# Reordering the first loads and splits, the last tile's gate, and the loads of stored activations and gate chunks in a PEER decoder layer

## Chip, cores and metric

One NeuronCore of a Trainium2 chip runs the kernel; the metric is the device time of one execution in microseconds (us), as the median of several runs. The profile is one further execution, taken by the hardware profiler.

## What is computed

One layer of a decoder for 512 prompt rows and 64 sample rows of width 1024, in float32. The layer is a combined input projection, attention and a spatial gating unit, an expert layer (PEER), and a last gate. Cut to what the change touches:

```python
xn = rmsnorm(x);  z = xn @ w_in                 # q, k, v, su, sv, two gates
...                                              # attention, gating unit, merge -> x1
q = rmsnorm(x1) @ w_q                            # 8 heads, scores against 2 x 128 sub keys
idx, gate = top16 of the 128 x 128 experts       # per row and head
w = gate * gelu(sum(u[idx] * rmsnorm(x1)))
x2 = x1 + sum(w * v[idx])                        # u, v: 16384 experts x 1024
gate2 = sigmoid(rmsnorm(x2) @ w_ple_gate)
x3 = x2 + gate2 * (p @ w_ple)
```

## The kernel before

**Precision.** Every float32 product is made of three fp32r matmuls. `split` (line 65) writes the high half of an operand with an activation copy on ACT and the rest with a subtraction on DVE. `load_block` (line 69) loads a weight block of 512 KB into `w_raw` (4 buffers), and splits it into `w_hi` and `w_lo` (3 buffers each). `tform` (line 78) runs high x high, high x low, low x high for each of eight blocks of 128 input rows, accumulating in a PSUM bank.

**Order.** The program text is not the order in which the engines run. A planner puts the instructions of each engine's queue in order while it works through a model of the run. Of those whose inputs and buffers are free it takes the one that stands first in the text; `tc.high_priority(offset=n)` moves an instruction n places ahead in that ranking. A load whose buffer is free can thus be issued long before its place in the text. Each queue then runs strictly in the order it was given. All plain loads and stores are issued by SP.

**Head** (lines 169 to 197). SP loads a small vector tile, then x transposed in eight blocks `xT` of 128 x 576, with the first block of `w_in` after the second of them, then `ident`. For each block ACT squares it and DVE adds the square into `tot` (`add`, ranked 500 ahead). ACT makes `xn[0]` (the high half of x times the norm's gain) and DVE `xn[1]` (the rest). `rstd_rows` turns `tot` into `rn`, the reciprocal norm of each column. `w_chunk` c multiplies `w_in` block c with all of x in two column halves (`HALVES`, 256 and 320 columns), one after the other, each in one of the two `mm` banks of PSUM, and DVE multiplies the result by `rn` on its way out. Nine small constants are loaded between chunk 0 and chunk 1. There are 30 chunks.

**Middle.** After the merge, the top-16 search runs mainly on DVE while TensorE does stage 1: for each expert block j of 128 (`stage1`, line 762) the activations of all 128 experts of that block for 384 prompt rows. The activations of j = 2, 4, ..., 38 (`SPILL`) are written to DRAM (`ad`), those of 43 others stay on chip. `build_g` (line 799) builds the dense gate of every expert and row and stores it in DRAM (`gd`). The other 192 rows get their experts by row gathers on GpSimd.

**Stage 2** (lines 943 to 985). For j = 0 to 127: load the block of `peer_v`, multiply the activations of block j by the gate (line 974, on DVE), split them into `wh` and `wl` (2 buffers each), and run 18 matmuls into six `oacc` banks (`stage2`, line 935). While stage 1 blocks are left, one is run beside; for j below 40 beside every second block. At block j the spilled activations of block j + 2 are loaded from `ad` into one of three `x1c` buffers (line 946). Every eighth block the gate of eight blocks (1.5 MB) is loaded as one chunk `gsl` (line 966); two chunks have a buffer.

**Tail** (lines 986 to 1027). Five row tiles are normalized, turned by TensorE (`tail_turn`, through `mm` banks) and multiplied by `w_ple_gate`. In `tail_gate` (line 898) the two column halves of 512 take turns, 48 matmuls in all. `tail_out` (line 905) then loads the tile's `pl`, and for each half takes the sigmoid on ACT, two DVE operations, and stores.

Of the kernel before, what the change touches and what calls it, by code (L numbers as in the profile page):

```python
# [7 lines left out]
F32 = mybir.dt.float32  # L8
# [3 lines left out]
AF = mybir.ActivationFunctionType  # L12
ALU = mybir.AluOpType
# [4 lines left out]
P = 128  # L18
D = 1024
NT = 576  # L20
NB = 384
KC = 8
NS = 64
NJ = 128
TB = 16
JB = 8
GP = [0.5, 0.0, 1.65]
G2 = (1.6, 2.0)
SPILL = set(range(2, 40, 2))
# [12 lines left out]
HALVES = (slice(0, 256), slice(256, 576))  # L42
# [5 lines left out]
def tile_decoder_step(ctx: ExitStack, tc: tile.TileContext, a, o):  # L48
    nc = tc.nc
    V, A, T, G, S = nc.vector, nc.scalar, nc.tensor, nc.gpsimd, nc.sync  # L50
# [9 lines left out]
    def cload(name, shape, pl=None):  # L60
        t = (pl or const).tile(shape, F32, name="c_" + name, bufs=1)
        S.dma_start(t, a[name])
        return t

    def split(src, hi, lo):
        A.activation(hi, src, AF.Copy)  # L66
        V.tensor_sub(lo, src, hi.bitcast(F32))  # L67

    def load_block(src, shape=(P, KC, P)):
        raw = wp.tile(list(shape), F32, name="w_raw", bufs=4)  # L70
        S.dma_start(raw, src)
        hi = wp.tile(list(shape), F32R, name="w_hi", bufs=3)
        lo = wp.tile(list(shape), F32R, name="w_lo", bufs=3)
        with tc.high_priority(offset=1000):
            split(raw, hi, lo)
        return hi, lo

    def tform(ps, w, x, wk=0, nk=KC):
        n, i = 3 * nk, 0
        for k in range(nk):  # L80
            for wi, xi in ((0, 0), (0, 1), (1, 0)):
                mark_pe[0] = T.matmul(ps, lhsT=w[wi][:, wk + k, :], rhs=x[xi][k], start=i == 0,  # L82
                                   stop=i == n - 1)
                i += 1
# [7 lines left out]
    def mm():  # L92
        return psM.tile([P, 512], F32, name="mm")
# [7 lines left out]
    pld = dr.tile([NT, D], F32, name="pld")  # L101
    ad = dr.tile([NSP, P, NB], F32, name="ad")
    gd = dr.tile([NJ // JB, P, NB // TB, JB, TB], F32, name="gd")
# [15 lines left out]
    def f8(mk, *args):  # L119
        t = [mk(*args), mk(*args)]  # L120
        return [t[k // 4][:, k % 4, :] for k in range(KC)]
# [4 lines left out]
    def bank(tag):  # L126
        return psB.tile([P, 512], F32, name=tag)

    def joint(w, x, out, wk=0, nk=KC, bk=mm):
        for cols in HALVES:  # L130
            ps = bk()[:, :cols.stop - cols.start]
            tform(ps, w, [[xi[k][:, cols] for k in range(nk)] for xi in x], wk, nk)
            out(ps, cols)

    def sumsq():
        tot = e1.tile([P, NT], F32, name="rstd", bufs=1)

        def add(k, x):
            sq = tt() if k else tot
            A.activation(sq, x, AF.Square)  # L140
            if k:
                V.tensor_tensor(tot, tot, sq, op=ALU.add)
            if k == KC - 1:
                A.activation(eps[:, 2:3], sq[:, 0:1], AF.Sqrt)
        return tot, add
# [22 lines left out]

    vecs = cload("vecs", [P, 18])
    xT = f8(f4)  # L170
    for k in range(KC):
        S.dma_start(xT[k], a["xT"][k])
        if k == 1:
            first = load_block(a["w_in"][0])
    ident = cload("ident", [P, P])
    xn = (f8(x4), f8(x4))
    tot, add = sumsq()
    for k in range(KC):
        with tc.high_priority(offset=500):
            add(k, xT[k])  # L180
        A.activation(xn[0][k], xT[k], AF.Copy, scale=vecs[:, k:k + 1])  # L181
        V.scalar_tensor_tensor(xn[1][k], xT[k], vecs[:, k:k + 1], xn[0][k].bitcast(F32),
                               op0=ALU.mult, op1=ALU.subtract)
    rn = e1.tile([P, NT], F32, name="rn", bufs=1)
    with tc.high_priority(offset=500):
        for cols, ps in rstd_rows(tot, lambda: bank("sc")):
# [2 lines left out]
    def w_chunk(c, dst, out):  # L189
        def scaled(ps, cols):  # L190
            with tc.high_priority(offset=1000):
                V.tensor_tensor(dst[:, cols], ps, rn[:, cols], op=ALU.mult)
            out(cols)
        joint(load_block(a["w_in"][c]) if c else first, xn, scaled)

    kraw, vTr = tt(), tt()
    w_chunk(0, kraw, lambda cols: None)
# [40 lines left out]
    for g in range(4):  # L238
# [7 lines left out]
        if g == 0:  # L246
            pv = bank("pt")
# [3 lines left out]
            pv = bank("pt")  # L251
# [206 lines left out]
    for i in range(24):  # L458
        if i < 8:
            t, g = (svT, suT)[i // 4], i % 4  # L460
            z = t[:, g, :]
            w_chunk(6 + i, z, lambda cols: A.activation(z[:, cols], z[:, cols], AF.Gelu_apprx_tanh))
        else:
            c, br = divmod(i - 8, 2)
            if (i - 8) % 4 == 0:
                sg4.append(f4())
            sg = sg4[-1][:, (i - 8) % 4, :]
# [15 lines left out]
    hs = ([], [])  # L483
    for c in range(KC):
        w = load_block(a["w_br"][c])
        for i, (x, k0_) in enumerate(((ahl, 0), (mhl, 4))):
            sg = sgs[2 * c + i]
# [20 lines left out]
    for c in range(KC):  # L508
        w = load_block(a["w_out"][c])
# [18 lines left out]
    for c0, r in tilesA:  # L528
# [4 lines left out]
        for hh in range(2):  # L533
            hs = slice(hh * 512, (hh + 1) * 512)
            pt = bank("pt")
            for k in range(4):
                x1k = x1[hh * 4 + k][:, c0:c0 + r]
                T.transpose(out=pt[:r, k * P:(k + 1) * P], in_=x1k, identity=ident)
                if r == NS:
# [3 lines left out]
                                   op0=ALU.mult, op1=ALU.mult)  # L543
# [186 lines left out]
    for i in range(16):  # L730
        h, c = i // 4 + i % 2 * 4, i // 2 % 2
        w = load_block(a["peer_wq"][2 * h + c])
# [17 lines left out]
    def pay(x):  # L750
        credit[0] += x
        n = int(credit[0])
        credit[0] -= n
        gather(n, mark_pe[0])
# [42 lines left out]
    gsp = [pool(gs_s, "gsp%d" % i, 1) for i in range(2)]  # L797
# [40 lines left out]
    for tb in range(NB // TB):  # L838
        if tb == TBK:
# [7 lines left out]
            g0 = late.tile([P, JB, TB], F32, name="g0")  # L847
# [19 lines left out]
    d3 = pool(ds, "d3", 3)  # L867
    gsp = [pool(ds, "gsl%d" % i, 1) for i in range(2)]
# [26 lines left out]
    def tail_scale(x2, ss, r, xn3):  # L895
        V.scalar_tensor_tensor(xn3[:r], x2[:r], ss[:r], pg[:r], op0=ALU.mult, op1=ALU.mult)

    def tail_gate(w, xh, xl, r, ps):
        for k in range(KC):
            for xi, wi in ((xh, 0), (xh, 1), (xl, 0)):  # L900
                for hh in range(2):
                    T.matmul(ps[hh][:r], lhsT=xi[:, k, :r], rhs=w[k][wi][:, hh * 512:(hh + 1) * 512],  # L902
                             start=k == 0 and xi is xh and wi == 0, stop=k == KC - 1 and xi is xl)

    def tail_out(x2, r, c0, ps, sg, pl):
        S.dma_start(pl[:r], pld[c0:c0 + r])
        for hh in range(2):
            hs = slice(hh * 512, (hh + 1) * 512)
            A.activation(sg[:r, hs], ps[hh][:r], AF.Sigmoid)
            V.tensor_tensor(sg[:r, hs], sg[:r, hs], pl[:r, hs], op=ALU.mult)  # L910
            V.tensor_tensor(sg[:r, hs], sg[:r, hs], x2[:r, hs], op=ALU.add)
            S.dma_start(o["y"][c0:c0 + r, hs], sg[:r, hs])
# [27 lines left out]
                                      start=j == 0 and last == 0 and vi is vh, stop=j == NJ - 1 and last == 1)  # L940

    tails, spp, back = [], [], {}
    for j in range(NJ):
        if j + 2 in SPILL:
            back[j + 2] = d3.tile([P, NB], F32, name="x1c")
            S.dma_start(back[j + 2], ad[sorted(SPILL).index(j + 2)])
        if j and j - 1 not in SPILL and j1 < NJ:
            stage1()
        pay(G2[0] if j1 < NJ else G2[1])
        if j == TAIL0:  # L950
            aLs.close()
            xds.close()
            spp.append(pool(sps, "spare", 2, "right"))
            gather(max(0, P - done[0]), mark_pe[0])
            pg = gp.tile([P, D], F32, name="xr")
            S.dma_start(pg, a["ple_g"])
            tails.append(gathered(0))
        if j == TAIL1:
            gather(1000, mark_pe[0])
        if j == NJ - 2:  # L960
            tails.append(gathered(1))
        if j % JB == 0:
            gsl = gsp[(j // JB + 1) % 2].tile([P, NB // TB, JB, TB], F32, name="gs")
            nb = NB // TB if j else NB // TB - 1
            with tc.high_priority(offset=0 if j else 300):
                S.dma_start(gsl[:, :nb], gd[j // JB][:, :nb])
            if j == 0:
                A.activation(gsl[:, nb], g0, AF.Copy)
        vw = load_block(pv_view[j], (P, D))
        wf = acts.pop(j)  # L970
        if j in SPILL:
            wf = back.pop(j)
        wfv = wf.rearrange("p (b t) -> p b t", t=TB)
        V.tensor_tensor(wfv, wfv, gsl[:, :, j % JB, :], op=ALU.mult)
        wh = d2.tile([P, NB], F32R, name="wh")
        wl = d2.tile([P, NB], F32R, name="wl")
        split(wf, wh, wl)
        held.append((j, wh, wl, *vw))
        if j != NJ - 2:
            for t in range(3):  # L980
                for hj in held:
                    stage2(t, *hj)
            held.clear()
        if max(SPILL) < j <= max(SPILL) + KC:
            add_x1(j - max(SPILL) - 1)
    ds.close()
    rows.close()
    tw = pool(ctx, "tw", 3)
    ws = []
# [3 lines left out]
    for t in range(3):  # L993
        x2 = tw.tile([P, D], F32, name="x2")
        xn3 = tw.tile([P, D], F32, name="xn3")
        ss = tw.tile([P, 2], F32, name="ss")
        for hh in range(2):
            hs = slice(hh * 512, (hh + 1) * 512)
# [12 lines left out]
    banks = [[mm(), mm()]] + [[psC.tile([P, 512], F32, name="oacc") for _ in range(2)] for _ in range(4)]  # L1011

    def finish_tile(i, x2, xh, xl, sg, r, c0):
        tail_gate(ws, xh, xl, r, banks[i])
        tail_out(x2, r, c0, banks[i], sg, tw.tile([P, D], F32, name="pl"))

    finish_tile(0, *tails[1])
    for t, (x2, xn3, ss) in enumerate(xs):
        xhl = xp.tile([P, 2, KC, P], F32R, name="x4")
        xh, xl = xhl[:, 0], xhl[:, 1]  # L1020
# [108 lines left out]
```

## Time and profile before

| | |
|---|---|
| median of 3 runs | 1782.91 us (1781.59 to 1785.38) |
| profiled execution, its own time | 1776.88 us |
| its span in the trace | 1775.1 us, 27763 instructions |
| TensorE matmul busy | 1744.3 us (98%) |
| DVE, ACT, GpSimd busy | 1434.0, 867.0, 525.9 us |
| bytes moved | 457.06 MB |

The profiled execution is 6.0 us below the median of the runs. Times in the rows are microseconds from the start of the span. PE is TensorE's matmul, DVE the vector engine, ACT the scalar engine, SPq the queue that issues loads and stores. "L82" is a line of the kernel. In brackets stands how long an engine was idle before the row and what ended the wait.

### The profile page before, as it was taken

How to read it: one execution, taken by the hardware profiler on the slowest of the kernel's cores; microseconds unless marked ns; L12 is line 12 of the kernel's file. 1: busy time of each engine (PE TensorE's matmuls, PEld its weight loads, DVE VectorE, ACT ScalarE, POOL GpSimd, SP SyncE). 2: the span in 40 equal slices, each digit the busy share in tenths (PEclk: the TensorE clock that was granted, in tenths of full speed). 3: DMA queues.
4: the chain of work that ended last, by engine and by line, in shares of the span. 5: the costliest groups of instructions: out<-in, count | busy, mean ns of one | idle time of the engine just before them, and what ended most of it. 6: DMA issues, size and time to landing. Idle time of an engine off the chain costs nothing.

```text
span 1775.1 us, 27763 instructions
## 1 busy us (share of the span) xinstructions
PE 1744.3 (98%) x10094; PEld 1575.1 (89%) x10094; DVE 1434.0 (81%) x2876; ACT 867.0 (49%) x1525; POOL 525.9 (30%) x390
## 2 busy tenths in 40 slices
PE   7999999999999899999999999999999999999998
PEld 7988999999999899999988887899899899887876
DVE  6455556548999999999898888998888888999862
ACT  6567444343236698999833333333333333333441
POOL 0000000000002112455245554454544554566300
PEclk9999999999999999999999999999999999999999
DMA  7211233443226577999999999999999999999741
GB/s 242 75 60 38 71 105 122 141 152 106 81 92 225 173 244 235 361 350 355 352 388 367 371 388 364 394 410 369 365 338 360 364 334 331 335 379 376 284 132 70
DMA packets 176457, 457.06 MB, mean 257 GB/s; under 512 B 15552, under 2 KB 76736, under 8 KB 174272
## 3 DMA queue, kind: packets, MB, share of 16 engines
q1 hardware_dynamic: 120736, 253.22, 40.6%
q0 software_dynamic: 55584, 202.07, 30.8%
q8 instruction: 79, 1.29, 0.3%
q14 instruction: 58, 0.48, 0.1%
HBM read 420.18 MB, written 35.78 MB: 257 GB/s over the span
## 4 chain that ended last, share of the span: by engine, by line
PE 77%; issue 7%; DVE 6%; DMA 5%; POOL 3%; ACT 1%; SPq 0%; DVEq 0%; POOLq 0%; ACTq 0%
PE mm L82 36%; PE oacc L939 21%; PE pv L82 5%; POOL row L707 3%; PE sc L822 2%; DMA row<-peer_v,idx 2%; PE pt L822 2%; PE oacc L902 2%; DVE w_lo L67 2%; PE sc L82 1%; DMA x1c<-ad 1%; DVE row L719 1%; DMA row<-peer_u,idx 1%; PE sc L580 1%; PE pv L447 1%
## 5 line engine op out<-in xcount | busy, mean ns | idle before, releaser
L66 ACT ACTIVATE w_hi<-w_raw 128x1024 fp32r<-128x1024 f32 x325 | 343.9, 1059 | 372.9 <-PE mm L82 287.1
L707 POOL DMA_INDIRECT row<-peer_u,idx x192 | 261.1, 1360 | 872.0 <-issue 520.8
L67 DVE TENSOR_TENSOR w_lo<-w_raw,w_hi 128x1024 fp32r<-128x1024 f32 x325 | 396.6, 1221 | 74.0 <-ACT w_hi L66 73.7
L82 PE MATMUL mm<-xd,w_hi 128*128 128x384 f32 x1552 | 405.9, 341 | 0.5 <-ACT w_hi L66 0.5
L82 PE MATMUL mm<-x,w_hi 128*128 128x256 f32 (+1 forms) x1600 | 329.7, 300 | 9.8 <-ACT x L181 9.5
L707 POOL DMA_INDIRECT row<-peer_v,idx x192 | 263.3, 1372 | 231.8 <-DVE acc L726 202.8
L82 PEld LDWEIGHTS mm<-xd,w_hi 128*128 128x128 f32 x1552 | 281.6, 189 | 5.9 <-ACT w_hi L66 0.8
L82 PEld LDWEIGHTS mm<-x,w_hi 128*128 128x128 f32 x1600 | 257.8, 190 | 24.1 <-ACT x L181 10.0
L82 PE MATMUL mm<-xd,w_lo 128*128 128x384 f32 x776 | 264.4, 341 | 3.7 <-DVE w_lo L67 3.7
L726 DVE SCALAR_TENSOR_TENSOR acc<-row,wts,acc 128x1024 f32<-128x1024 f32 x192 | 245.8, 1280 | 5.3 <-DMA row<-peer_v,idx 4.9
L939 PE MATMUL oacc<-w_hi,wl 128*128 128x512 f32 x768 | 242.0, 397 | 3.7 <-DVE wl L67 3.6
L939 PE MATMUL oacc<-w_lo,wh 128*128 128x512 f32 x768 | 242.0, 396 | 0.4 <-DVE w_lo L67 0.4
L939 PE MATMUL oacc<-w_hi,wh 128*128 128x512 f32 x768 | 242.3, 396 | 0.0
L719 DVE SCALAR_TENSOR_TENSOR row<-row,xr 128x1024 f32<-128x1024 f32 x192 | 231.6, 1221 | 11.0 <-DMA row<-peer_u,idx 8.6
L82 PE MATMUL mm<-x,w_lo 128*128 128x256 f32 (+1 forms) x800 | 236.6, 296 | 0.0
L939 PEld LDWEIGHTS oacc<-w_hi,wl 128*128 128x128 f32 x768 | 144.3, 188 | 39.6 <-DVE wl L67 5.5
L939 PEld LDWEIGHTS oacc<-w_lo,wh 128*128 128x128 f32 x768 | 144.4, 188 | 35.5 <-DVE w_lo L67 1.7
L939 PEld LDWEIGHTS oacc<-w_hi,wh 128*128 128x128 f32 x768 | 143.7, 188 | 29.4 <-ACT xr L921 0.8
L82 PEld LDWEIGHTS mm<-x,w_lo 128*128 128x128 f32 x800 | 151.7, 190 | 1.1 <-issue 0.8
L82 PEld LDWEIGHTS mm<-xd,w_lo 128*128 128x128 f32 x776 | 147.0, 189 | 4.7 <-DVE w_lo L67 4.7
L82 PE MATMUL pv<-xd,w_hi 128*128 128x384 f32 x496 | 136.7, 348 | 0.7 <-ACT x L776 0.7
L66 ACT ACTIVATE wh<-x 128x384 fp32r<-128x384 f32 x66 | 34.7, 526 | 162.6 <-PE oacc L939 153.1
(304 smaller groups left out, 2308.8 us busy)
## 6 DMA issues: line engine op xcount, KB each, us to landing
w_raw<-peer_uT SPq DMA_DIRECT2D x128, 512.0 KB
w_raw<-peer_v SPq DMA_DIRECT2D x128, 512.0 KB
gd<-gs SPq DMA_DIRECT2D x24, 1024.0 KB
gs<-gd SPq DMA_DIRECT2D x15, 1536.0 KB
w_raw<-w_in SPq DMA_DIRECT2D x30, 512.0 KB
w_raw<-peer_wq SPq DMA_DIRECT2D x16, 512.0 KB
w_raw<-w_br SPq DMA_DIRECT2D x8, 512.0 KB
w_raw<-w_out SPq DMA_DIRECT2D x8, 512.0 KB
```

Source lines behind the costliest of these rows:

```text
L66: A.activation(hi, src, AF.Copy)
L67: V.tensor_sub(lo, src, hi.bitcast(F32))
L82: mark_pe[0] = T.matmul(ps, lhsT=w[wi][:, wk + k, :], rhs=x[xi][k], start=i == 0, stop=i == n - 1)
L447: T.matmul(ps[:r], lhsT=xi[:, k, :r], rhs=wl_[k][wi][:, hh * 512:(hh + 1) * 512], start=i == 0, stop=i == 5)
L580: T.matmul(ps[:, b * P:(b + 1) * P], lhsT=qp[:, b * P:(b + 1) * P], rhs=sk, start=True, stop=True)
L707: ins = G.indirect_dma_start(out=row_, out_offset=None, in_=table, in_offset=bass.IndirectOffsetOnAxis(ap=ix, axis=0))
L719: V.scalar_tensor_tensor(row_, row_, 1.0, xrs[ti], op0=ALU.mult, op1=ALU.mult, accum_out=dots[:, s:s + 1])
L726: V.scalar_tensor_tensor(accs[ti], row_, wts[:, s:s + 1], accs[ti], op0=ALU.mult, op1=ALU.add)
L822: T.matmul(pt[:, t * P:(t + 1) * P], lhsT=oa[:, t, :], rhs=ob[:, t, :], start=True, stop=True)
L902: T.matmul(ps[hh][:r], lhsT=xi[:, k, :r], rhs=w[k][wi][:, hh * 512:(hh + 1) * 512], start=k == 0 and xi is xh and wi == 0, stop=k == KC - ...
L939: mark_pe[0] = T.matmul(oacc[t][hh], lhsT=wi[:, ts], rhs=vi[:, hh * 512:(hh + 1) * 512], start=j == 0 and last == 0 and vi is vh, stop=j = ...
```

## The change

It has four parts. First, the head: block 0 of `w_in` is loaded ahead of x, block 1 behind x, then `ident`, then block 2 (whose split is no longer ranked ahead), all ahead of the constants. The products `xn` are ranked 1500 ahead, and the squares follow in a loop of their own (500). Chunk 0 runs both column halves together, input block by input block. Chunk 1 uses the `pv` banks of PSUM, chunk 2 the `pt` banks. Second, the tail: the last tile's gate runs as 512 columns, then 256, then 256, each with its own sigmoid and store; the last 256 go into `banks[0][0]`, the first `mm` bank of the first tile. The load of `pl` stands ahead of the gate. Third, the spilled activations of block j + 4 are loaded at block j (those of 2 and 4 at block 0). Fourth, chunk c + 1 of the gate is loaded in four quarters, at blocks 1, 3, 5 and 7 of chunk c.

```diff
-    def load_block(src, shape=(P, KC, P)):
+    def load_block(src, shape=(P, KC, P), urgent=True):
...
-        with tc.high_priority(offset=1000):
+        with tc.high_priority(offset=1000 if urgent else 0):
             split(raw, hi, lo)
...
+    first = [load_block(a["w_in"][0])]
     for k in range(KC):
         S.dma_start(xT[k], a["xT"][k])
-        if k == 1:
-            first = load_block(a["w_in"][0])
+    first.append(load_block(a["w_in"][1]))
     ident = cload("ident", [P, P])
+    first.append(load_block(a["w_in"][2], urgent=False))
...
     for k in range(KC):
-        with tc.high_priority(offset=500):
+        with tc.high_priority(offset=1500):
+            A.activation(xn[0][k], xT[k], AF.Copy, scale=vecs[:, k:k + 1])
+            V.scalar_tensor_tensor(xn[1][k], xT[k], vecs[:, k:k + 1], xn[0][k].bitcast(F32),
+                                   op0=ALU.mult, op1=ALU.subtract)
+    with tc.high_priority(offset=500):
+        for k in range(KC):
             add(k, xT[k])
-        A.activation(xn[0][k], xT[k], AF.Copy, scale=vecs[:, k:k + 1])
-        V.scalar_tensor_tensor(xn[1][k], xT[k], vecs[:, k:k + 1], xn[0][k].bitcast(F32),
-                               op0=ALU.mult, op1=ALU.subtract)
...
-        joint(load_block(a["w_in"][c]) if c else first, xn, scaled)
+        w = first[c] if c < 3 else load_block(a["w_in"][c])
+        if c:
+            joint(w, xn, scaled, bk=(mm, lambda: bank("pv"), lambda: bank("pt"))[c] if c < 3 else mm)
+            return
+        pss = [mm()[:, :cols.stop - cols.start] for cols in HALVES]
+        for k in range(KC):
+            for ps, cols in zip(pss, HALVES):
+                for i, (wi, xi) in enumerate(((0, 0), (0, 1), (1, 0))):
+                    T.matmul(ps, lhsT=w[wi][:, k, :], rhs=xn[xi][k][:, cols], start=k == 0 and i == 0,
+                             stop=k == KC - 1 and i == 2)
+        for ps, cols in zip(pss, HALVES):
+            scaled(ps, cols)
...
+    GB, chunks = NB // TB, [0]
+    def gate_chunk():
+        chunks[0] += 1
+        return gsp[chunks[0] % 2].tile([P, GB, JB, TB], F32, name="gs")
     for j in range(NJ):
-        if j + 2 in SPILL:
-            back[j + 2] = d3.tile([P, NB], F32, name="x1c")
-            S.dma_start(back[j + 2], ad[sorted(SPILL).index(j + 2)])
+        for jb in (2, 4) if j == 0 else (j + 4,):
+            if jb in SPILL:
+                back[jb] = d3.tile([P, NB], F32, name="x1c")
+                S.dma_start(back[jb], ad[sorted(SPILL).index(jb)])
...
+        elif j % JB == 0:
+            gsl = gnext
+        if j % JB % 2 and j // JB < NJ // JB - 1:
+            q = j % JB // 2
+            if q == 0:
+                gnext = gate_chunk()
+            qs_ = slice(q * GB // 4, (q + 1) * GB // 4)
+            S.dma_start(gnext[:, qs_], gd[j // JB + 1][:, qs_])
...
     def finish_tile(i, x2, xh, xl, sg, r, c0):
-        tail_gate(ws, xh, xl, r, banks[i])
-        tail_out(x2, r, c0, banks[i], sg, tw.tile([P, D], F32, name="pl"))
+        pl = tw.tile([P, D], F32, name="pl")
+        S.dma_start(pl[:r], pld[c0:c0 + r])
+        parts = list(zip(banks[i], (slice(0, 512), slice(512, D))))
+        groups = [parts]
+        if i == 4:
+            groups = [parts[:1], [(banks[i][1], slice(512, 768))], [(banks[0][0], slice(768, D))]]
+        for g in groups:
+            tail_gate(ws, xh, xl, r, g)
+            tail_out(x2, r, c0, sg, pl, g)
```

## Rows read from the trace of the kernel before

**Rows 1.** The page: busy time, share of the span and instructions of each engine
```profile
PE 1744.3 (98%) x10094; PEld 1575.1 (89%) x10094; DVE 1434.0 (81%) x2876; ACT 867.0 (49%) x1525; POOL 525.9 (30%) x390
```

**Rows 2.** Windows: stretch, length, busy (count) per engine, granted clock, DMA share, GB/s
```profile
0.00:9.18 9.18, 0.01 (x1) 0.01 (x1) 2.87 (x7) 5.11 (x7) 0.20 (x4) 1.00 0.77 255
9.18:22.50 13.32, 12.65 (x70) 10.67 (x70) 10.98 (x18) 12.81 (x23) 0.00 (x0) 1.00 0.65 225
...
512.00:865.00 353.00, 345.12 (x2179) 332.75 (x2177) 348.84 (x969) 290.87 (x620) 108.86 (x76) 0.99 0.82 275
...
1000.00:1135.00 135.00, 129.63 (x612) 110.76 (x610) 118.43 (x171) 45.47 (x61) 67.41 (x50) 1.00 0.97 378
...
1210.00:1526.00 316.00, 316.00 (x1590) 285.84 (x1589) 272.93 (x343) 111.68 (x152) 157.71 (x124) 1.00 0.95 347
```

**Rows 3.** Head, SP's queue: a wait (total, times, longest) and one constant's load
```profile
SPq L62 <- DMA c<-xT: 3.4, 6, 1.2
...
11.71 0.58 SPq L62 DMA_DIRECT2D c_maskS<-maskS  x1
```

**Rows 4.** Head, timeline of ACT and DVE: start, duration, what
```profile
4.19 0.68 ACT L140 ACTIVATE rstd<-c 128x576 f32<-128x576 f32 x1 [2.16 <-DMA c<-xT]
...
15.41 2.76 ACT L181 ACTIVATE x<-c,c_vecs 128x576 fp32r<-128x576 f32 x4
...
18.68 1.51 DVE L182 SCALAR_TENSOR_TENSOR x<-c,c_vecs,x 128x576 fp32r<-128x576 f32 x2
...
21.29 1.23 DVE L67 TENSOR_TENSOR w_lo<-w_raw,w_hi 128x1024 fp32r<-128x1024 f32 x1 [1.00 <-ACT w_hi L66]
...
22.61 0.42 ACT L187 ACTIVATE rn<-sc 128x320 f32<-128x320 f32 x1
```

**Rows 5.** Chain of waits, first 60 us: shares by line, then pieces with start and length
```profile
by line: PE mm L82 62.2%; DMA c<-xT 8.6%; ACT x L181 4.9%; PE sc L234 3.9%; ACT t L140 3.8%; PE sc L165 2.4%; ACT L144 2.1%; PE sc L151 2.0%; PE pv L216 1.6%; SPq L172 1.4%; DVE x L182 1.4%; DVE rstd L142 1.1%; issue 0.9%; PE pt L249 0.7%; 
...
29.52 0.97 PE pv L216 x4
30.49 6.35 PE mm L82 x48
```

**Rows 6.** Head, timeline of TensorE: two matmuls of one shape
```profile
12.38 0.41 PE L82 MATMUL mm<-x,w_lo 128*128 128x256 f32 x1
...
15.73 0.28 PE L82 MATMUL mm<-x,w_lo 128*128 128x256 f32 x1
```

**Rows 7.** Waits around stage 2: total, times, longest, of PE, DVE and SP
```profile
PE oacc L939 <- DVE wl L67: 3.6, 3, 1.3
PE mm L82 <- DVE w_lo L67: 2.5, 1, 2.5
...
DVE x1c L974 <- DMA x1c<-ad: 14.7, 9, 4.9
...
SPq L946 <- DVE wl L67: 25.6, 13, 3.3
```

**Rows 8.** Stage 2, timeline of SP's queue, ACT and DVE
```profile
1060.25 0.33 SPq L71 DMA_DIRECT2D w_raw<-peer_v  x1
...
1066.49 0.33 SPq L966 DMA_DIRECT2D gs<-gd  x1
...
1071.90 0.44 SPq L946 DMA_DIRECT2D x1c<-ad  x1
...
1072.74 1.06 ACT L66 ACTIVATE w_hi<-w_raw 128x1024 fp32r<-128x1024 f32 x1 [2.88 <-PE mm L82]
...
1081.44 0.56 DVE L974 TENSOR_TENSOR x1c<-x1c,gs 128x384 f32<-128x384 f32 x1 [4.91 <-DMA x1c<-ad]
```

**Rows 9.** End of the tail, timeline of ACT, DVE and SP's queue
```profile
1768.81 1.08 ACT L909 ACTIVATE xn<-oacc 128x512 f32<-128x512 f32 x2 [10.11 <-issue]
...
1770.65 1.29 DVE L911 TENSOR_TENSOR xn<-xn,x 128x512 f32<-128x512 f32 x2
1771.37 0.94 SPq L912 DMA_DIRECT2D out_y<-xn  x2
```

More of the change, by code (lines that the diff above doesn't have):

```diff
@@ L896, in tail_scale, with tail_gate, tail_out @@
         V.scalar_tensor_tensor(xn3[:r], x2[:r], ss[:r], pg[:r], op0=ALU.mult, op1=ALU.mult)
-    def tail_gate(w, xh, xl, r, ps):
+    def tail_gate(w, xh, xl, r, parts):
         for k in range(KC):
             for xi, wi in ((xh, 0), (xh, 1), (xl, 0)):
-                for hh in range(2):
-                    T.matmul(ps[hh][:r], lhsT=xi[:, k, :r], rhs=w[k][wi][:, hh * 512:(hh + 1) * 512],
+                for p, hs in parts:
+                    T.matmul(p[:r, :hs.stop - hs.start], lhsT=xi[:, k, :r], rhs=w[k][wi][:, hs],
                              start=k == 0 and xi is xh and wi == 0, stop=k == KC - 1 and xi is xl)
[L905 to L909, printed above, removed]
+    def tail_out(x2, r, c0, sg, pl, parts):
+        for p, hs in parts:
+            A.activation(sg[:r, hs], p[:r, :hs.stop - hs.start], AF.Sigmoid)
             V.tensor_tensor(sg[:r, hs], sg[:r, hs], pl[:r, hs], op=ALU.mult)
@@ L961, in tile_decoder_step @@
             tails.append(gathered(1))
[L962 to L968, printed above, removed]
+        if j == 0:
+            gsl = gate_chunk()
+            with tc.high_priority(offset=300):
+                S.dma_start(gsl[:, :GB - 1], gd[0][:, :GB - 1])
+            A.activation(gsl[:, GB - 1], g0, AF.Copy)
+        elif j % JB == 0:
[6 more added lines that the diff above has]
+            S.dma_start(gnext[:, qs_], gd[j // JB + 1][:, qs_])
         vw = load_block(pv_view[j], (P, D))
```

## The prediction

> **What bounds the kernel now.** I read the page first: TensorE is busy 98% of the span [rows 1], so a gain can only come from the 31 us in which it is not, or from work that runs slowly. The windows then say where these lie [rows 2]: nothing runs on it for the first 9.18 us; 353 us of the middle hold 7.9 us of idle time, with DVE busy 348.8 us of them; stage 2 has 5.4 us of idle time between 1000 and 1135, and none at all from 1210 to 1526. Three places are touched by the change: the head, the stalls of stage 2, and the end after the last matmul. The middle is not touched, but everything in it follows from what came before, so a gain of the head should go through it as a shift.
>
> **The head.** In the stretch from 9.18 to 22.5, ACT is busy 12.81 of 13.32 us [rows 2], with squares and `xn` taking turns. The constants' loads wait six times for a block of x to land [rows 3]; I read the last of these waits, which ends at 11.71, as the landing of the last block. Its `xn` is ready much later: DVE ends the last one at 18.68 + 1.51 = 20.19 [rows 4]. That is the lag that the change attacks.
>
> After the change the same bytes (block 0 and all of x) stand ahead of the last landing, so I keep 11.71. One `xn` high half takes ACT 2.76 / 4 = 0.69, one rest takes DVE 1.51 / 2 = 0.75 [rows 4]: the last block is ready at 11.71 + 0.69 + 0.75 = 13.15 if nothing stands in front. TensorE needs 6.35 / 8 = 0.79 for one of eight input blocks of a chunk [rows 5], which gives 13.95 as the earliest end of chunk 0. Its early matmuls are slow, though: the granted clock reads 1.00 (the level of 2.4 GHz) in the whole stretch, yet a matmul of 256 columns takes 0.41 at 12.38 and 0.28 at 15.73 [rows 6]; before the slow one TensorE had been at work, with gaps, since 9.18. If the slow time after the first matmul is as long as here (at least 3.2 us, at most 6.5), a start near 6.6 (the first block of x now lands behind 0.52 MB of weights, at 4.19 + 1.5 = 5.7; then ACT's 0.69 and what is left of block 0's split) means slow matmuls until about 12, at some 1.2 to 1.5 us for each input block. About three blocks are then done, and five at 0.79 end near 16. I take 15.5. The late end is 17.5: squares placed between the `xn` on ACT (eight of 0.68 [rows 4]) put the last `xn` near 16.6.
>
> Now the chain: chunk 1 ends at 29.52 before, and `rstd_rows` has put 2.0% + 2.4% of 60 us = 2.6 us of small matmuls ahead of that [rows 5]. After: 15.5 + 2.6 + 6.35 = 24.5, so 5.0 us earlier; with the ends 13.95 and 17.5 it is 6.6 and 3.1. What is late next is block 2's split, ranked behind the squares: ACT has eight squares (5.4 us) from about 14, a table load and then the split, and DVE's half takes 1.23 [rows 4], so it comes at 21.5 to 23 while chunk 2 wants it near 22 to 24. I charge 0.5 us (0 to 1.5). `rn` moves later with the squares: it ends at 22.61 + 0.42 = 23.0 before [rows 4], after eight squares that were spread out; all squares behind the `xn` cost at most 5.4 us more, so 28.4. It was needed at once before, as chunk 0's banks had to be emptied for chunk 1. With three chunks in three pairs of banks it is needed when chunk 3 starts, near 31. **Head: -4.5 us, from -6.6 to -1.5.** The moved constants cost nothing: their first users come after chunk 0, and SP waits among them today anyway.
>
> **The tail.** After the last matmul ACT takes two sigmoids (1.08), then DVE four operations; the last ends at 1770.65 + 1.29 = 1771.94, 3.13 us after 1768.81 [rows 9]. With 256 columns last, one sigmoid, one multiplication and one addition remain: 0.54 + 0.65 + 0.65 = 1.84 if they did not shrink, 0.92 if they halved; the multiplication is taken to cost what the addition of its shape does. I take 1.2, gain 1.9. The last store is issued earlier by that and half as long; I take another 0.2 (0 to 0.4). TensorE pays little for 72 matmuls in place of 48, as the columns are the same: 48 matmuls of 288 columns on average take 6.35, 0.132 each [rows 5], so 256 alone cost about 0.12; I charge 0.1. The bank lent to the last tile leaves `tail_turn` one `mm` bank in place of two until the end; its six steps lie beside gates of two other tiles, so I charge 0.2 (0 to 1). The earlier `pl` load has slack. **Tail: -1.8 us, from -2.5 to -0.5.**
>
> **The spilled activations.** The trace shows what a late one costs: a load issued at 1071.90, behind a chunk of 1.5 MB issued at 1066.49, lets DVE wait 4.91 us until 1081.44 [rows 8]; TensorE then waits 2.5 us for `w_lo`. Three later waits for `wl` cost 3.6 [rows 7], as DVE has fallen behind. But SP does not issue these loads late because of their place in the text. In 13 cases it waits for DVE's `wl` to free one of the three `x1c` buffers [rows 7]. With three buffers, block j + 4 takes the buffer of block j - 2, whenever it stands in the text. So the part gives nothing where the buffer decides: **0 us, from -6.1 (both kinds of stall gone) to the price of the rival below.**
>
> **The gate chunks.** The same holds for the quarters: all four need the one buffer that the last product of an older chunk frees, and the planner then issues all that is free. The chunk of 1066.49 was not needed by TensorE for many blocks. I expect four loads back to back, the same bytes in the same order, and SP busy 3 x 0.33 us longer for a chunk. **0 us**; cover is SP's idle time.
> Weighed against the row: blocks of 288 KB of x, queued one behind the other, and block 0 land between 4.19 and 11.71, 2.59 MB in 7.52 us, 344 GB/s [rows 3, 4]; stage 2 with mostly 512 KB loads moves 378 GB/s [rows 2]. The Trainium skill's page "DMA: Bandwidth & Descriptors" (section "Measured (HBM→SBUF, 128 partitions, SWDGE, issued from GpSimd)") speaks against the change: loads should be batched to 1 MiB or more. It measured loads issued from GpSimd; these come from SP, so the trace neither confirms nor refutes it. It stands behind the third rival.
>
> **Sum.** -4.5 - 1.8 = -6.3 us. The profiled execution would take 1776.88 - 6.3 = 1770.6. The runs' median is 6.0 above it, and I carry the difference over: 1782.91 - 6.3 = **1776.6**. A difference of 0.2%, 3.6 us, is about what a measurement of this kernel can tell from no change.
>
> **Rivals.**
> First, stage 2 gains too: SP gets the load of block j + 4 ahead of the weight loads of block j, so it no longer queues behind them, and the 6.1 us of waits go. Then 1770.5. For it: at 1071.90 the load came after weight loads that SP had waited for. Against it: the buffer waits. 0.17.
> Second, the head does not do what it says: the planner's model lands x late, fills ACT with squares between the `xn`, chunk 0 ends at 17.5 or later and block 2 is late too; -1.5 with the tail's -1.8 gives 1779.6. For it: that is just how ACT's queue looks now. Against it: `xn` now outranks the squares by 1000. 0.18.
> Third, smaller loads move fewer bytes: 1.57 MB at 344 in place of 378 GB/s takes 0.41 us more for a chunk; about seven chunks lie in the stretch where DMA is busy 97% [rows 2], 2.9 us in all: 1779.5. By the page's rule it would go this way. 0.05.
> Fourth, the other side, slower. SP's queue is strictly in order. If the load of block j + 4 gets its earlier place literally, ahead of a weight load, SP stands still until `wl` of block j - 2 is done, with three weight loads behind it. A weight load issued at 1060.25 is used at 1072.74, 12.5 us later, and the slow landing above took 9.5: 3.0 us of slack [rows 8]. Standing one weight load (12.5 / 3 = 4.2 us) earlier, SP would hold the next by up to 4.2, 1.2 more than the slack. It decides from a hold of 3.0 us; SP's longest is 3.3 today [rows 7]. Ten of the 19 spilled blocks would cost 12 us: 1788.6. Against it: the planner today places these loads by free buffers. 0.1.
> That leaves 0.5 for the forecast, whose own range is 1773 to 1780.
>
> **How the numbers follow.** Faster by over 0.2% means below 1779.3. The forecast gives 0.46 of its 0.5 to it, the first rival all of 0.17, the second 0.05, the third 0.02: 0.70. Slower takes 0.08 of the fourth. The rest, 0.22, is the same. The range must reach to the first and second rival and take in the bounds of the head: 1769.5 to 1781.5; the fourth rival is left out.
>
> **What would show it.** In the head: the first matmul near 6.6, the last `xn` near 13 to 14 with squares after it, chunk 0 done by 16, and the first chunk of 48 matmuls after the `pv` sums some 4 to 5 us earlier. In the tail: about 1.2 us from the last matmul to the last addition, against 3.13. In stage 2: the same waits of DVE for `x1c` (14.7 us) and of SP for `wl`, and four quarter loads within 2 us. The forecast is wrong if TensorE waits for `w_lo` of block 2 or for `rn`, if its idle time in the middle (7.9 us) changes by more than 2 us because the planner chose other orders, or if stage 2's idle time changes by more than 2.

## The result

| | kernel before | changed kernel |
|---|---|---|
| median of 9 runs each | 1781.59 us (1779.09 to 1785.38) | 1789.51 us (1787.21 to 1796.38) |
| ratio, 95% interval | | 1.0054 (1.0038 to 1.0071) |
| profiled execution, its span | 1776.88, 1775.1 us | 1795.46, 1793.7 us |

The change makes the kernel 8 us slower; 1776.6 was forecast, with a range up to 1781.5. The profiled execution of the changed kernel is 6 us above its median, so the losses read from it are that much larger than those of a middle run.

The page of the changed kernel (busy time, share, instructions), then its chain of waits in the head with the same piece in the kernel before, then the end of the tail:

```profile
PE 1752.2 (98%) x10118; PEld 1582.4 (88%) x10118; DVE 1434.6 (80%) x2878; ACT 868.8 (48%) x1526; POOL 531.8 (30%) x390
```
```profile
40.83 6.46 PE mm L82 x48
```
```profile
44.52 6.46 PE mm L82 x48
```
```profile
1789.40 0.39 ACT L921 ACTIVATE xn<-mm 128x256 f32<-128x256 f32 x1 [2.38 <-PE mm L916]
1789.82 0.43 DVE L922 TENSOR_TENSOR xn<-xn,pl 128x256 f32<-128x256 f32 x1 [1.88 <-ACT xn L921]
1790.28 0.43 DVE L923 TENSOR_TENSOR xn<-xn,x 128x256 f32<-128x256 f32 x1
```

Head and tail did what was forecast: the chunk that ran from 44.52 runs from 40.83, 3.7 us earlier, and the last addition ends 1.34 us after the last matmul (1789.37), where it took 3.13 [rows 9]. The loss lies between. Three windows of stage 2 (stretch, length, busy time of PE, PEld, DVE, ACT, POOL, granted clock, DMA share, GB/s), and the waits of TensorE for DVE and of DVE for the loads (total, times, longest):

```profile
880.00:1000.00 120.00, 115.10 (x541) 100.11 (x542) 102.61 (x116) 41.45 (x56) 61.33 (x41) 0.99 0.96 357
1000.00:1140.00 140.00, 132.19 (x612) 113.32 (x611) 118.60 (x170) 46.58 (x62) 69.82 (x49) 0.98 0.96 363
1140.00:1220.00 80.00, 71.97 (x355) 64.15 (x354) 62.74 (x100) 22.18 (x31) 37.40 (x27) 0.94 0.96 360
```
```profile
PE mm L82 <- DVE w_lo L67: 15.7, 7, 4.1
PE oacc L951 <- DVE w_lo L67: 4.8, 3, 4.2
```
```profile
DVE x L998 <- DMA gs<-gd: 16.8, 5, 6.4
DVE x1c L998 <- DMA x1c<-ad: 15.6, 7, 6.4
DVE aL L998 <- DMA gs<-gd: 5.5, 2, 3.8
...
DVE x1c L998 <- DMA gs<-gd: 4.2, 1, 4.2
```

TensorE's waits are those of the whole span; 14.1 of the 15.7 us lie in these windows. TensorE stands for 340 - 115.10 - 132.19 - 71.97 = 20.7 us of these 340, 18.9 of them behind DVE's `w_lo`. Before, the large waits were 2.5 us for `w_lo` and 3.6 for `wl` [rows 7]. DVE now waits 26.5 us for `gs`, the gate chunks, against 0.5 before. One such place, on SP's queue, DVE and TensorE:

```profile
1163.28 0.82 SPq L992 DMA_DIRECT2D gs<-gd  x2
...
1164.89 0.33 SPq L71 DMA_DIRECT2D w_raw<-peer_v  x1
1165.27 0.59 SPq L992 DMA_DIRECT2D gs<-gd  x1
1165.96 0.41 SPq L890 DMA_DIRECT2D x1c<-x1d  x1
...
1166.43 0.66 SPq L992 DMA_DIRECT2D gs<-gd  x1
...
1178.68 0.56 DVE L998 TENSOR_TENSOR x<-x,gs 128x384 f32<-128x384 f32 x1 [6.43 <-DMA gs<-gd]
1179.16 1.22 DVE L67 TENSOR_TENSOR w_lo<-w_raw,w_hi 128x1024 fp32r<-128x1024 f32 x1
...
1180.43 1.22 PE L951 MATMUL oacc<-w_lo,wh 128*128 128x512 f32 x2 [4.22 <-DVE w_lo L67]
1181.45 1.05 PE L951 MATMUL oacc<-w_hi,wl 128*128 128x512 f32 x2
```

The four quarters are issued with a weight load and an `x1c` load between them; the last one lands 12 us after its issue. DVE stands 6.43 us before a product of that chunk. It is not this product that TensorE waits for, but the split that TensorE needs next stands behind it in DVE's line, and TensorE waits 4.22 us. Afterwards two matmuls take 1.05 us instead of 0.63; from 1180 to 1200 the mean granted clock is 0.84.

### The profile page after: what moved, and what is told of

The parts are those of the page before. It is cut to its first block, busy times and chain, and to the rows that moved or that the text cites. A ratio compares the mean times of both kernels' runs of the same rounds, so it can differ in the third digit from the quotient of the medians.

```text
span 1793.7 us, 27904 instructions
## 1 busy us (share of the span) xinstructions
PE 1752.2 (98%) x10118; PEld 1582.4 (88%) x10118; DVE 1434.6 (80%) x2878; ACT 868.8 (48%) x1526; POOL 531.8 (30%) x390
## 4 chain that ended last, share of the span: by engine, by line
PE 78%; DVE 8%; DMA 6%; issue 5%; POOL 2%; ACT 1%; SPq 0%; DVEq 0%; POOLq 0%; ACTq 0%
PE mm L82 36%; PE oacc L951 22%; PE pv L82 5%; DMA gs<-gd 4%; PE oacc L916 2%; PE sc L836 2%; PE pt L836 2%; DVE w_lo L67 2%; DMA row<-peer_v,idx 2%; POOL row L721 2%; PE sc L82 1%; DVE row L733 1%; PE sc L594 1%; PE pv L461 1%; PE mm L916 1%
## 5 line engine op out<-in xcount | busy, mean ns | idle before, releaser
L721 POOL DMA_INDIRECT row<-peer_u,idx x192 | 265.9, 1385 | 877.0 <-issue 518.0
L82 PE MATMUL mm<-x,w_hi 128*128 128x320 f32 (+1 forms) x1504 | 306.8, 298 | 0.0
L82 PE MATMUL mm<-xd,w_lo 128*128 128x384 f32 x776 | 267.0, 344 | 15.7 <-DVE w_lo L67 15.7
L82 PEld LDWEIGHTS mm<-x,w_hi 128*128 128x128 f32 x1504 | 240.4, 189 | 12.5 <-issue 9.0
L82 PE MATMUL mm<-x,w_lo 128*128 128x320 f32 (+1 forms) x752 | 221.2, 294 | 0.0
L82 PEld LDWEIGHTS mm<-x,w_lo 128*128 128x128 f32 x752 | 141.8, 189 | 1.1 <-issue 0.8
```

The lines of the kernel that those rows point to most:

```text
L721: ins = G.indirect_dma_start(out=row_, out_offset=None, in_=table, in_offset=bass.IndirectOffsetOnAxis(ap=ix, axis=0))
```

## Experiments

Times are medians; in brackets stands the ratio to the kernel before, measured beside each, with its 95% interval. The kernel before took 1779.1 to 1779.8 us there.

### Which of the four parts

The whole chunk in place of the quarters (the fourth part undone):

```diff
-        if j % JB % 2 and j // JB < NJ // JB - 1:
-            ...
-            S.dma_start(gnext[:, qs_], gd[j // JB + 1][:, qs_])
+        if j % JB == 0:
+            ...
+                S.dma_start(gsl[:, :nb], gd[j // JB][:, :nb])
```

> The changed kernel with its fourth part undone: every gate chunk is one load of 1.5 MB at the first block of its chunk, as before; head, tail and the spilled activations two blocks further ahead stay. The changed kernel lost about 13.6 us somewhere: 1789.5 measured, against 1781.6 less the 3.7 of the head and the 2.0 of the tail that its trace shows, 1775.9. Theory A (the quarters: DVE stands 26.5 us waiting for them in stage 2): 1776, no wait of DVE for gs over 1 us, TensorE's idle time from 890 to 1220 back at a few us. Rival B (the spilled activations' earlier place): stays near 1789. Rival D (the head moved every later order, neither load matters): stays near 1789.

Measured: **1765.5 us (0.992, 0.9905 to 0.9934)**, faster than either kernel. TensorE's idle time from 880 to 1220 is 0.8 us:

```profile
880.00:1000.00 120.00, 119.71 (x570) 103.96 (x571) 110.79 (x126) 43.92 (x60) 58.01 (x44) 1.00 0.99 384
1000.00:1140.00 140.00, 139.47 (x674) 121.51 (x673) 128.59 (x190) 49.56 (x66) 73.50 (x54) 1.00 1.00 394
1140.00:1220.00 80.00, 80.00 (x421) 72.71 (x420) 70.81 (x109) 26.76 (x36) 39.05 (x30) 1.00 1.02 401
```
```profile
PE 1740.9 (99%) x10118; PEld 1574.8 (89%) x10118; DVE 1435.4 (81%) x2878; ACT 868.1 (49%) x1526; POOL 523.0 (30%) x390
```

Between the two profiled executions lie 31.4 us: 19.9 of idle time in these windows, and 11.3 because the same 10118 matmuls take 1752.2 us instead of 1740.9. They run slower after stalls: in the 10 to 12 us from the ends of the changed kernel's four longest stalls on (957, 1091, 1152 and 1180; 3.7 to 4.2 us each) the granted clock is 0.69 to 0.83, while with whole chunks it is 1.00 in all three windows. So the quarters are the cause, but 1776 had been expected; the next three kernels split the rest. The third part undone (`back[j + 2]` at block j again), quarters kept:

> The changed kernel with its third part undone: the spilled activations of block j + 2 are loaded at block j, as before; head, tail and quarters stay. Theory A (the quarters): stays near 1789, DVE waits some 25 us for gs. Rival B (the spilled activations): 1776, and DVE's waits for gs go. Rival D (orders shifted by the head): near 1789 with this one and with the whole chunks alike.

Measured: 1796.8 (1.0098, 1.0083 to 1.0113). That is far from rival B's 1776, so the quarters stay the cause. DVE waits 15.5 us for `gs` and not some 25, but the profiled execution was the fastest of this kernel's (1788.55). The time lies above theory A's 1789, too: the third part is seen to *help*, and without it the changed kernel is 7 us slower still. Third and fourth part both undone:

> The head and the tail of the change alone: whole chunks at the first block, spilled activations of block j + 2 as before. By the traces of the changed kernel the head gives 3.7 us and the tail 2.0: 1779.1 less 5.7 is 1773.4, and the spilled activations two blocks further ahead are then worth the other 7.9 of the 13.6 us that the kernel with whole chunks gained. Rival: the 13.6 us come from another order that the head leaves to stage 2, and the spilled activations give nothing (my forecast): 1765.5 here too.

Measured: 1773.2 (0.9959, 0.9945 to 0.9973), 6.7 us faster than before; my sum for head and tail was 6.3. The rival's 1765.5 falls. And the kernel before with the third part alone (`for jb in (2, 4) if j == 0 else (j + 4,)`):

> The kernel before with the third part alone: the spilled activations of block j + 4 loaded at block j. If it clears stage 2 of its idle time (6.7 us between 1000 and 1140 in the trace of before): 1772, with DVE's waits for x1c (14.7 us) down to some 8 as in the kernel with whole chunks. If the buffers decide when these loads are issued, as I forecast: 1779, the waits as before.

Measured: 1772.0 (0.9952, 0.9934 to 0.997), 7.8 us faster. The parts add up: -6.7 - 7.8 = -14.5 against the -13.6 of the kernel with whole chunks; the quarters then cost 1789.5 - 1765.5 = 24 us. How the third part gains is seen where a chunk is loaded. SP's queue and DVE before, then with the third part alone:

```profile
935.90 0.33 SPq L966 DMA_DIRECT2D gs<-gd  x1
937.03 0.33 SPq L71 DMA_DIRECT2D w_raw<-peer_v  x1
939.62 0.33 SPq L946 DMA_DIRECT2D x1c<-ad  x1
941.95 0.33 SPq L71 DMA_DIRECT2D w_raw<-peer_v  x1
...
951.57 0.56 DVE L974 TENSOR_TENSOR x1c<-x1c,gs 128x384 f32<-128x384 f32 x1 [2.67 <-DMA x1c<-ad]
```
```profile
937.67 0.33 SPq L967 DMA_DIRECT2D gs<-gd  x1
941.98 0.33 SPq L947 DMA_DIRECT2D x1c<-ad  x1
942.36 2.29 SPq L71 DMA_DIRECT2D w_raw<-peer_v  x2
...
950.67 0.61 DVE L975 TENSOR_TENSOR x1c<-x1c,gs 128x384 f32<-128x384 f32 x1 [0.25 <-DMA x1c<-ad]
```

Both `x1c` loads leave when DVE's `wl` has freed the buffer (its end at 939.60 and 941.95). But a weight load that stood ahead now stands behind. DVE's next wait for `x1c` is 0.25 us instead of 2.67, and over stage 2 these waits fall from 14.7 us [rows 7] to 6.9. Such exchanges are nearly all that differs: TensorE, ACT and GpSimd have the same order of instructions in both kernels, SP's differs in 14 of 518 places, seven exchanges of an `x1c` load with a weight load ahead of it, and DVE's in 7, all before 915 us. Where such a load stands behind a chunk it landed 11.0, 10.6, 12.3 and 10.1 us after its issue with head and tail alone, and 8.0, 7.9, 8.7 and 6.8 with the third part added.

### Place or pieces

One load, at block 1 of the chunk before:

```diff
-        if j % JB % 2 and j // JB < NJ // JB - 1:
-            ...
+        if j % JB == 1 and j // JB < NJ // JB - 1:
+            gnext = gate_chunk()
+            S.dma_start(gnext, gd[j // JB + 1])
```

> The changed kernel, but the gate of chunk c + 1 is one load of 1.5 MB at block 1 of chunk c: the early place in the text without the four pieces. Theory A1 (the pieces: four short loads, ranked between weight loads, finish late on the chip while DVE's products already stand in line for them): 1776. Rival A2 (the early place: the load goes ahead of weight loads that are needed sooner): 1789.

Four loads, at the first block of the chunk itself:

```diff
+        elif j % JB == 0:
+            gsl = gate_chunk()
+            for q in range(4):
+                qs_ = slice(q * GB // 4, (q + 1) * GB // 4)
+                S.dma_start(gsl[:, qs_], gd[j // JB][:, qs_])
```

> The changed kernel, but all four quarter loads of a chunk stand at its first block, where the one load stood before: the pieces without the early place. Theory A1 (the pieces): 1789, with waits of DVE for gs of 20 us or more. Rival A2 (the early place): 1776.

Measured: 1765.5 (0.9923, 0.991 to 0.9935) and 1790.8 (1.006, 1.0047 to 1.0073). The place in the text does nothing, as forecast: the buffer decides. The pieces do it all. Theory A1 is right in kind, though its 1776 lacked the gain of the third part, and DVE's waits for `gs` with four loads are 18.8 us, where 20 or more had been expected. SP's queue and DVE around one chunk, first with one load (the kernel with whole chunks), then with four:

```profile
932.26 0.33 SPq L979 DMA_DIRECT2D gs<-gd  x1
936.58 0.33 SPq L959 DMA_DIRECT2D x1c<-ad  x1
936.95 2.29 SPq L71 DMA_DIRECT2D w_raw<-peer_v  x2
...
944.98 0.55 DVE L987 TENSOR_TENSOR x1c<-x1c,gs 128x384 f32<-128x384 f32 x1
945.45 0.55 DVE L987 TENSOR_TENSOR x<-x,gs 128x384 f32<-128x384 f32 x1
```
```profile
934.94 0.80 SPq L989 DMA_DIRECT2D gs<-gd  x2
936.08 0.33 SPq L71 DMA_DIRECT2D w_raw<-peer_v  x1
936.45 0.71 SPq L989 DMA_DIRECT2D gs<-gd  x1
937.89 0.32 SPq L964 DMA_DIRECT2D x1c<-ad  x1
938.26 0.44 SPq L989 DMA_DIRECT2D gs<-gd  x1
...
951.88 0.56 DVE L995 TENSOR_TENSOR x1c<-x1c,gs 128x384 f32<-128x384 f32 x1 [6.03 <-DMA x1c<-ad]
954.19 0.56 DVE L995 TENSOR_TENSOR x<-x,gs 128x384 f32<-128x384 f32 x1 [1.75 <-DMA gs<-gd]
```

The `x1c` product is that of a spilled block of the chunk before (at 951.88 it starts before this chunk is complete); the `x` product behind it is the first of the new chunk. With one load DVE comes to these two 12.7 and 13.2 us after SP issued the chunk, and both find their data. With four DVE is at the `x1c` product after 10.9 us. It stands there 6.03 us, as the spilled block's load was issued behind three quarters and a weight load, and then 1.75 us for the last quarter, which lands 19.2 us after the first was issued. So the quarters cost twice: by their own late end, and by what they push back. DVE's waits for `x1c` are 14.9 us with four loads and 8.3 with one.

### Why four cost more than one

Two causes were possible on SP's side, the shorter runs of a quarter (3 KB per partition instead of 12) and the number of loads. Four loads of 32 whole partitions each (`gsl[ps_]`, `gd[j // JB][ps_]`, ps_ a quarter of the partitions):

> As the kernel with four loads at the first block of the chunk (1790.8), but each load takes 32 partitions whole (12 KB in one run for each) in place of a quarter of every partition (3 KB runs on 128 partitions). Same number of loads, same bytes, same place. Theory P (the run's length: while one 1.5 MB load was under way, the queue of SP's loads moved 2.28 MB in 10.1 us against 1.65 MB of the row gathers; with quarters 1.57 to 2.00 MB in 10 us against 1.8 to 2.1 MB: a queue with short packets loses its share to the gathers, and the weight loads behind it land late): 1766, no wait of DVE for gs over 1 us. Theory N (the number of loads: the order that the planner gives them among the weight loads, and DVE's products that it places too soon): 1790, DVE waiting some 15 to 25 us for gs.

Measured: 1879.0 (1.0563, 1.0536 to 1.0591). Neither theory allows that; the run answers nothing about them, since its own cost is far larger (last section). One load with runs of 3 KB:

```diff
+        raw = gsp[chunks[0] % 2].tile([P, 4, GB // 4 * JB * TB + PAD], F32, name="gs")
...
+            S.dma_start(gsl, gd[j // JB].rearrange("p (q b) j t -> p q (b j t)", q=4))
```

> As the kernel with one whole load at the first block of the chunk (1765.5), but the chunk's buffer has 32 bytes of padding behind each quarter, so that the one load writes runs of 3 KB. Theory P (the run's length): 1790, and landing later than the 10.1 us of the whole load. Theory N (the number of loads): 1766, landing near 10.

Measured: 1770.1 (0.9946, 0.9928 to 0.9965). Every engine has the same order of instructions as with 12 KB runs (only the first chunk's load is in two), so the 4.6 us are the runs' own price (the two intervals just overlap, so it may be less). Issues of the chunk with 12 KB and with 3 KB runs (count, size, median us to landing):

```profile
gs<-gd SPq DMA_DIRECT2D x15, 1536.0 KB, 10.1
```
```profile
gs<-gd SPq DMA_DIRECT2D x15, 1536.0 KB, 13.1
```

Landing at 13.1 is still about when DVE comes. Most of the 24 us is left for the number of loads, and here an idea that I had fell: that DVE's products stand earlier in its order with quarters. TensorE, ACT and GpSimd have the same order of instructions with one load and with four, and DVE's differs in 27 of 2878, all at the start of stage 2. What differs throughout is SP's order. So the quarters were pulled together in it (`tc.high_priority(offset=5000 if j > 2 * JB else 0)` around the four loads):

> As the kernel with four loads at the first block of the chunk (1790.8), but from the third chunk on the quarters are ranked 5000 ahead, so that SP issues all four one behind the other, as it issues the one load. DVE's order is the same in both, instruction by instruction; before, one weight load of 512 KB and one load of a spilled block stood between the quarters. Theory O (SP's order: the last quarter lands late because 0.7 MB of other loads stand ahead of it, and DVE's line, which does not change, runs into it): near the one load with 3 KB runs, 1771 (1769 to 1775), DVE's waits for gs 2 to 3 us. Theory N (four loads cost more than one wherever they stand, for example by four landings to wait for): stays near 1790.

Measured: 1775.6 (0.9986, 0.9974 to 0.9998), 15 us less, with the same order on every engine but SP. SP now issues the quarters together:

```profile
933.92 2.39 SPq L990 DMA_DIRECT2D gs<-gd  x4
936.81 0.57 SPq L964 DMA_DIRECT2D x1c<-ad  x1
```

Theory O explains the larger part, but not down to 1771: DVE still waits 5.5 us for `gs`, where 2 to 3 had been expected, and 14.8 for `x1c`. The first two of the fifteen chunks that come in quarters pulled together as well:

> As the kernel whose quarters stand together from the third chunk on (1775.6), but for every chunk, the first two included. What is left open is the 5.5 us between that kernel and the one load with 3 KB runs (1770.1). Theory O (SP's order alone, the first two chunks being the rest): 1770 (1768 to 1773). Theory N (each of four loads costs something of its own): stays near 1776.

Measured: 1775.4 (0.9974, 0.9961 to 0.9986): no. Some 5 us belong to four loads as such. One thing in the trace comes with them: SP stands before weight loads until some earlier load has landed, here for 28.7 us between 880 and 1240 (total, times, longest), against 3.3 us with one load of 12 KB and 7.5 with one of 3 KB. It does not explain the time, though: the kernel at 1775.6 above, which is as fast, has 12.6 us of them. What the 5 us are stays open.

```profile
SPq L71 <- DMA w_raw<-peer_v: 13.1, 3, 5.1
SPq L71 <- DMA gs<-gd: 9.6, 8, 1.8
SPq L71 <- DMA w_raw<-peer_uT: 6.0, 3, 4.0
```

### Products ahead of need

DVE multiplies resident activations with the gate up to eight blocks ahead. Held back, these products can't stand before a late quarter:

```diff
+        ins = V.tensor_tensor(wfv, wfv, gsl[:, :, j % JB, :], op=ALU.mult)
+        if j >= 3:
+            after(ins, marks[j - 3])
```

> As the kernel with four loads at the first block (1790.8), but the planner may place the product of block j with the gate only after the matmuls of block j - 3. Until now DVE takes products up to eight blocks ahead, the first ones right behind the landing of their chunk. Theory D (the loss is DVE standing before products that nobody needs yet): DVE's waits for gs go, and the time comes near the one load with 3 KB runs, 1770 (1768 to 1776). Theory Q (the loss is in SP's queue: weights and spilled blocks land late, whatever DVE does): 1784 or more. The hold itself may cost or gain; the next kernel measures it.

> The same hold with one whole load for a chunk (1765.5 without the hold). If the products that run ahead are worth nothing, 1765.5 again; if DVE needs them as filling for its gaps, more: by TensorE's waits in the kernel with whole chunks (2 to 3 us in stage 2) not below 1763.

Measured: 1781.9 (1.0013, 1.0003 to 1.0022) with four loads, 1785.2 (1.0028, 1.0018 to 1.0039) with one. The time with four is in neither theory's range. But with the hold four loads cost nothing more than one, DVE's waits for `gs` are down to 0.6 us in the kernel with four, and its TensorE has no idle time from 880 to 1526. So the loss of the quarters does go through DVE's line. But the hold costs the kernel with whole chunks 19.7 us: from 1526 to 1700 TensorE is busy 156.57 us there, against 173.98 without it, and its waits are

```profile
PE oacc L951 <- ACT wh L66: 13.2, 10, 2.5
PE oacc L951 <- DVE wl L67: 4.1, 4, 1.6
```

The products done early are work that DVE has little time for later: it is busy 159.9 of these 174 us, against 151.5 without the hold. Last, the quarters really spread over blocks 1, 3, 5 and 7:

```diff
-            S.dma_start(gnext[:, qs_], gd[j // JB + 1][:, qs_])
+            after(S.dma_start(gnext[:, qs_], gd[j // JB + 1][:, qs_]), mark_pe[0])
```

> The changed kernel (1789.5), but each quarter load may be placed only after the last matmul that stands ahead of it in the text, so that SP issues the four some twelve us apart, at blocks 1, 3, 5 and 7, as the text has them. Theory O or D (late quarters hold up a line that does not wait for blocks): 1768 to 1772, as a quarter delays the loads behind it by 0.38 MB in place of 1.5. If short runs cost the same wherever they stand: 1770, as the one load with 3 KB runs. If four loads cost more than one wherever they stand: near 1790.

Measured: 1818.0 (1.0216, 1.0192 to 1.0241), outside all I had written. SP does spread them (925.48, 938.89, 951.56, 963.98), and TensorE stands only 4.9 us between 880 and 1220. But a chunk is complete only with its last quarter, so DVE can't work ahead. From 1526 to 1700 TensorE is busy 150.28 of 174 us and waits 19.0 for ACT's `wh`. That fits the cost of the hold, and no run separates the two.

## Why the prediction was wrong

**Head, -4.5: right.** Measured 3.7. The first matmul is at 6.50 (6.6), the matmuls are slow until 11.83 (12), the last `xn` ends at 13.74 (13 to 14), `rn` at 28.33 (28.4), and no one waits for block 2. Chunk 0 ends at 16.06, half a microsecond later than I took. (The late end of the range is misadded: 3.1 less 1.5 is 1.6.)

**Tail, -1.8: right.** Measured 2.0 from the last matmul to the end of the span; its own size 1.34 us (1.2). (The late end, by its own terms, is 3.13 - 1.84 - 0.1 - 1 = 0.2 and not 0.5; neither slip moves the stated range.) Head and tail together gave 6.7 us in the run with these two alone.

**Spilled activations, 0: wrong, -7.8.** The step that failed is "the part gives nothing where the buffer decides". The buffer decides when the load is issued, and it did; it does not decide what is queued ahead of it. The part moves a weight load of 512 KB behind it. My fourth rival saw that very thing, SP standing still with weight loads behind it, and priced it as a loss at 3.0 us of slack. SP's waits at this load grew from 25.6 us [rows 7] to 41.5 with whole chunks, the longest from 3.3 to 5.5, and no loss came of it. The first rival was the true one: it said that these loads would no longer queue behind weight loads. It had 6.1 us for it. Stage 2's idle time was my sign, and it did move: 6.7 us before from 880 to 1220, 3.5 with the third part alone.

**Gate chunks, 0: wrong, +24.** "The same bytes in the same order" failed twice. The planner gives each load its own place, and puts other loads between them: the four that I wanted to see within 2 us are issued over 3.2 us at the place shown. And "the chunk was not needed by TensorE for many blocks" was true of TensorE and not of DVE, whose line held the first product of a chunk 9 to 13 us behind its issue. Where that product stands in DVE's line I had not asked. The "cover" that I named, SP's idle time, was not what had to hold: the slack was that of the landing against DVE's line. With whole chunks DVE comes 2.7 us after the landing at the place around 932 (13.2 less 10.5). At the chunk before whose product it waits 6.43 us in the changed kernel, it has no slack at all: with whole chunks that chunk is issued at 1139.52, and DVE waits 0.29 us for it. My third rival priced only the rate of smaller loads, +2.9 us, for seven chunks in a stretch in which five are issued; the runs of 3 KB cost 4.6. The Trainium skill's page "DMA: Bandwidth & Descriptors" (section "Measured (HBM→SBUF, 128 partitions, SWDGE, issued from GpSimd)") wants loads of 1 MiB or more, for the rate. The time went its way, but the trace does not show its reason: the DMA engines moved 394 GB/s while one load of 1.5 MB was under way (932.2 to 944 with whole chunks), and 394 while four of 0.38 MB were (934.9 to 954.5 with four loads).

**The middle** was to be wrong if its idle time changed by more than 2 us. TensorE is busy 344.92 us in the 353 from 508.3 on, against 345.12 in the same stretch before, 3.7 us later [rows 2]: no new loss there.

## What to carry to other kernels

When a load is cut in pieces, ask where each piece will stand in the queue and which strictly ordered engine meets the last piece first; the slack is that of the landing against this engine's line, not against the engine that bounds the kernel. A load whose start is fixed by its buffer can still gain or lose by what is queued ahead of it. Work that an engine does ahead of need may be what keeps it in time later, so a fix that takes it away must be priced as well.

## What the hardware showed

Loads of 32 partitions are slow for everyone. The kernel with four of them for each chunk, from 927.90 to 940.40 (40 slices; busy share of the DMA engines in tenths, then GB/s); such loads are moving up to 929.8 (one issued at 920.46) and again from 934.5 on (one issued at 927.94):

```profile
DMA  9896799999999999999999999979999989989799
GB/s 184 157 170 118 144 249 275 320 392 374 413 408 400 408 419 406 419 419 419 406 433 446 315 262 184 236 144 197 184 223 210 210 184 223 262 223 249 210 328 341
```

The engines stay busy, but while such a load moves they carry mostly 118 to 275 GB/s instead of some 400. Between 880 and 1240 a packet of 12 KB takes 824 ns on average, against 471 in loads of 128 partitions (whole chunks), and a packet of 4 KB of the gathers 210 against 166. Row gathers lose as well: DVE waits 39.6 and 35.9 us for them between 880 and 1240, against 8.4 and 0.7 with whole chunks. The Trainium skill's page "DMA: Bandwidth & Descriptors" (section "🎯 Rules for kernel authors") advises one load of 128 partitions in place of two of disjoint halves, because both use the same engines. The trace agrees that it doesn't pay, here for four loads of 32 partitions: 1879 us, against 1790.8 with four of 128.
